# Moving tile addresses in SBUF so that the two operands of each product lie at different residues modulo 256 bytes

## The chip, the cores and the metric

The kernel runs on one core of one Trainium2 chip. A core has five engines with queues of their own: TensorE (PE, matrix products; the profile lists its weight loads as PEld), VectorE (DVE), ScalarE (ACT), GpSimd (POOL) and SyncE (SP, which mostly issues DMAs). On-chip memory is SBUF, 128 partitions, and PSUM, into which TensorE accumulates. The metric is the device time of one execution in microseconds (us).

A product on TensorE has two operands in SBUF. The stationary one (128 columns here) is put into the array by a LDWEIGHTS instruction; the moving one (up to 512 columns) is then streamed past it by a MATMUL. While one MATMUL streams, the LDWEIGHTS of the next one runs beside it.

## What is computed

One layer of a hybrid decoder trunk on 512 tokens of width 1024, in float32:

```python
h = rms_norm(x, g_pre_mix)
z = h @ w_in
y_a = gmlp_mixer(gelu(u), gelu(v), ...)      # spatial gating in chunks of 128 tokens
y_b = nsa_mixer(q, k_cmp, v_cmp, ...)        # 16 heads, 4 KV groups: compressed, selected, window
y_c = rglru_mixer(xr, rg, ...)               # convolution of width 4, linear recurrence
merged = gates[0] * (y_a @ w_br_a) + gates[1] * (y_b @ w_br_b) + gates[2] * (y_c @ w_br_c)
x = x + rms_norm(merged @ w_o, g_post_mix)
f_gate, f_up = split(rms_norm(x, g_pre_ffn) @ w_ffn_in)
return x + rms_norm((silu(f_gate) * f_up) @ w_ffn_out, g_post_ffn)
```

## The kernel before

**Products.** Nearly all the work is matrix products in the type fp32r. Each float32 operand is split into a high part (`hi`, rounded to fp32r by ACT) and a low part (`lo`, the rest, by DVE), by `split` (lines 131 and 136). A product is then three: `hi`x`hi`, `hi`x`lo`, `lo`x`hi`. `passes` (line 259) runs them over the eight blocks of 128 of the inner dimension, with the weight as stationary operand and 512 tokens as moving operand: 24 MATMULs of 512 columns. `v_pair` (line 857) does the opposite: 128 tokens of `hh`/`hl` are stationary, and 256 columns of the weight tile move. Line 614 (`v_half`), line 1496 (`wo_pass`) and line 1876 (`down`) also move weights, in 512 columns. Some large products are done on quarters of the matrices, with sums formed beforehand, in 256 columns: line 1260 (`b_pair`, two of the three branches) and line 1740 (`product_parts`, the FFN's input). Attention uses line 941 (scores: `q` stationary, `K` moving), line 966 (transposes of `P` with `ident`) and line 979 (values: `V` stationary, `ph`/`pl` moving).

**Order.** Python generators are interleaved by `run` and by the planner in `attention`; each yields between small groups of instructions, and so sets the order in which each engine's queue is filled. Waits follow from which tile an instruction reads or writes. In stage 1 (attention) groups of four transposes stand between the products; outside it, products mostly follow one another directly.

**Memory.** SBUF is cut into pools that are laid one behind the other: `const`, `mid` (with the `row` tiles), `stage` (`raw`, where weights land), `merge` (tag `m`), `wts` (the ring of `hi` and `lo`), `big` (tags `y` and `h`), then `early`, and above it a pool for each of three phases. A tile's address is the sum of the sizes ahead of it, each rounded up to 32 bytes. `slab` gives the large tiles. Those with the tags `y`, `mo`, `f` and `wab` are made longer than needed, and the argument `first` shifts the data in them by that many elements. `MOVED` is 16 elements, 64 bytes. With these sizes `mid`, `stage`, `merge`, `wts` and `big` all begin at a multiple of 256 bytes, and their large tiles too. The operands of a product then stand at these distances (address of the moving one minus that of the stationary one, modulo 256):

| product | before |
|---|---|
| 259, 701: `hh`, `gxh`, `yah` with `hi`/`lo` (512 columns) | 0 |
| 614, 1496, 1876 (512 columns, weights move), 498 | 0 |
| 857 `v_pair` (256 columns) | 0 |
| 941 scores, 979 values, 911 | 0 |
| 1260 branches (256 columns): `yc`, `yb`, `t` with `hi`, `lo`, rows | 64, some 192 |
| 259, 1598, 1740 FFN (256 columns): `fh`, `fl`, `t` with `hi`, `lo`, `u` | 64 |
| 259, 1598 with the rows `uh`, `ul` | 192 |

Of the kernel before, what the change touches and what calls it, by code (L numbers as in the profile page):

```python
# [24 lines left out]
F32 = mybir.dt.float32  # L25
F32R = mybir.dt.float32r
# [5 lines left out]
S = 512  # L32
D = 1024
NK = 8
# [18 lines left out]
def hybrid_block(ctx: ExitStack, tc: tile.TileContext, A, out):  # L53
    nc = tc.nc
    V, SC, GP, PE, SY = nc.vector, nc.scalar, nc.gpsimd, nc.tensor, nc.sync

    const = ctx.enter_context(tc.tile_pool(name="const", bufs=1))
# [44 lines left out]
    def slab(name, dt=F32, tag=None, shape=(4, S), first=0):  # L102
        pool, bufs = (merge if tag == "m" else big, TAGS[tag]) if tag in TAGS else phase_pool[tag]
        if tag not in ("y", "mo", "f", "wab"):
            return pool.tile([128, *shape], dt, tag=tag, name=nm(name), bufs=bufs)
        size = 2064 if tag == "f" else 2112
        t = pool.tile([128, size], dt, tag=tag, name=nm(name), bufs=bufs)[:, first:first + math.prod(shape)]
        return t if len(shape) == 1 else t.rearrange(
            "p (a b) -> p a b" if len(shape) == 2 else "p (a b c) -> p a b c", **dict(zip("abc", shape)))
# [28 lines left out]
    res = {}  # L138
# [134 lines left out]
    def const0(shape, name):  # L273
        return phase_pool["s0"][0].tile(shape, F32, name=name, bufs=1)
# [12 lines left out]
    sp4 = const0([128, 8], "sp4")  # L287
    spm8 = const0([128, 8], "spm8")
    lt = const0([128, 6, 8], "lt")
    const0([128, 8], "space")  # L290
    V.memset(ones, 1.0)
    warm = const.tile([128, 17], F32, name="warm")[:, 0:1]
    V.memset(warm, 0.0)
    SC.activation(warm, warm, AF.Exp)
    ident = const.tile([128, 128], F32, name="ident")
# [54 lines left out]

    gh, gl = Pair("gxh", F32R, "y"), Pair("gxl", F32R, "y")
    hh, hl = Pair("hh", F32R, "h"), Pair("hl", F32R, "h")

    def scaled(k):
# [96 lines left out]
    def load_wab():  # L453
        raw = slab("wabr", tag="s1", shape=(2, NK, 128))
        SY.dma_start(raw, A["wab"])
        hi = slab("wabh", F32R, "wab", (2, NK, 128), 48)
        lo = slab("wabl", F32R, "wab", (2, NK, 128), 48)
        wab["hi"], wab["lo"] = hi, lo
        for _ in range(4):
            yield  # L460
        for k in range(0, NK, 2):
            split(raw[:, :, k:k + 2], hi[:, :, k:k + 2], lo[:, :, k:k + 2])
            yield
# [198 lines left out]

    def u_tile(j):
        if j == 0:
            ya["h"], ya["l"] = Pair("yah", F32R, "y"), Pair("yal", F32R, "y")
        g = j // 2
        ps = bank("mm")
        yield from matrix(ps, hh, hl)
        u = row("u")
        gelu2(ps, u)  # L670
        yield
        pm = bank("tr")
        for c in range(4):
            PE.matmul(pm[:, c * 128:(c + 1) * 128], gm["v"][c // 2][:, c % 2, j * 128:(j + 1) * 128],  # L674
                      gm["ws"][:, g, :], start=True, stop=True)
        cb = gm["cb"][:, j % 2:j % 2 + 1]
        rwb = gm["rwb"]
        V.scalar_tensor_tensor(cb[:, 0], rwb[:, 0, g], half[:, 2, j:j + 1], rwb[:, 1, g],
                               op0=OP.mult, op1=OP.add)
        m = row("mix")  # L680
        V.scalar_tensor_tensor(m.rearrange("p (c t) -> p c t", c=4),
                               pm.rearrange("p (c t) -> p c t", c=4), half[:, 1, j:j + 1],
                               cb.to_broadcast([128, 4, 128]), op0=OP.mult, op1=OP.add)
        V.tensor_mul(m, m, u)
        split(m, ya["h"][j], ya["l"][j])
        yield
# [144 lines left out]
        yield  # L831

    def k_tile(g):
        K = slab("K", F32R, "k", (2, 2, S))
        at[g]["k"] = K
        ps = bank("mm")
        yield from matrix(ps, hh, hl)
        for br in range(2):
            src = ps[64 * br:64 * br + 64]
            for h in range(2):  # L840
                SC.activation(K[64 * h:64 * h + 64, 0, br, :], src, AF.Copy)
            for h in range(2):
                V.tensor_sub(K[64 * h:64 * h + 64, 1, br, :], src, f32(K[64 * br:64 * br + 64, 0, br, :]))
        yield

    def v_pair(n):

        us = [unit() for _ in range(2)]
        bs = [bank("mm") for _ in range(2)]
        for c in range(4):  # L850
            q = slice(c * 128, (c + 1) * 128)
            ps = bs[c // 2][:, c % 2 * 256:c % 2 * 256 + 256]
            for k in range(NK):
                hi, lo = us[k // 4]
                ws = slice(k % 4 * 256, k % 4 * 256 + 256)
                for t, (x, w) in enumerate(((hh, hi), (hh, lo), (hl, hi))):
                    PE.matmul(ps, x[k][:, q], w[:, ws], start=(k == 0 and t == 0), stop=(k == NK - 1 and t == 2))  # L857
                if k % 4 == 3:
                    yield
            if c == 1:  # L860
                while n == 1 and 1 not in done:
                    yield
                VV = slab("V", F32R, "v", (4, 2, 2, 2, 64))
                at["v", n] = VV
            if c % 2:
                src = bs[c // 2].rearrange("p (c g b d) -> p c g b d", c=2, g=2, b=2)
                for i in range(2):
                    v = VV[:, c - 1 + i]
                    SC.activation(v[:, :, :, 0, :], src[:, i], AF.Copy)
                    V.tensor_sub(v[:, :, :, 1, :], src[:, i], f32(v[:, :, :, 0, :]))  # L870
# [120 lines left out]
    def mask_in():  # L991
        mask[0] = slab("mask", tag="mask", shape=(S,))
        GP.memset(mask[0], 0.0)
        GP.affine_select(mask[0][:, 384:], mask[0][:, 384:], pattern=[[-1, 128]], compare_op=OP.is_ge,
                         fill=-1e30, base=0, channel_multiplier=1)

    def attention(fills):

# [84 lines left out]

    def yb_tile(name, tag, dt=F32):

        size = {"b1": 2048, "b21": 1024, "b22": 1064}[tag]
        return yb["at"].tile([128, size], dt, tag=tag, name=nm(name), bufs=1)[:, :2048 if tag == "b1" else 1024]

    class Tokens:
# [36 lines left out]
    def yb_rest():  # L1126

        (b11, b12), (b21, b22) = yb["y"].h

        def quarter(t):  # L1130
            return t.rearrange("p (k t) -> p k t", k=4)

        V.tensor_sub(b11, b22, b11)
        yield
        V.scalar_tensor_tensor(b22, b12, -1.0, b22, op0=OP.mult, op1=OP.subtract)
        yield
        t = slab("t", F32R, "f", (2, 4, 256), MOVED)
        yb["b"][2] = t[:, 0], t[:, 1]
        split(b11, *yb["b"][2])
        V.tensor_sub(b21, b21, b11)  # L1140
        yield
        t = yb_tile("t", "b1", F32R).rearrange("p (i k t) -> p i k t", i=2, k=4)
        yb["b"][3] = t[:, 0], t[:, 1]
        split(b22, *yb["b"][3])
        yield
        yb["b"][4] = quarter(yb_tile("t", "b22", F32R)), quarter(slab("t", F32R, "w2", (2048,))[:, :1024])
        split(b21, *yb["b"][4])
        yield
# [101 lines left out]
    def b_pair(p, x="b"):  # L1250
# [39 lines left out]
            return  # L1290
        if p % 2 == 0:
            for n in "hl"[:1 if p else 2]:
                mg.setdefault(n, []).append(slab("m" + n, F32R, "mo"))
        for j, r in ((2 * p, r1), (2 * p + 1, r2)):
            t, m = mg.pop(("b", j)), mg["m"][j]
            V.scalar_tensor_tensor(t, t, 1.0, r, op0=OP.add, op1=OP.mult)
# [6 lines left out]

    def low_late():

        mg["l"].append(slab("ml", F32R, "mo"))
        for j in (4, 5):
            V.tensor_sub(mg["l"][1][:, j - 4], mg["m"][j], f32(mg["h"][1][:, j - 4]))

# [121 lines left out]
    def rows_in():  # L1431
        gb = slab("gb", tag="gb", shape=(2, D))
        res["gb"] = gb
        x = yb_tile("x", "b1").rearrange("p (c n) -> p c n", c=2)
        res["x"] = [x[:, 0], x[:, 1], yb_tile("x", "b21"), yb_tile("x", "b22")]
        res["ss"] = const.tile([128, 4, 4], F32, name="ss")
        fh, fl = res["fh"], res["fl"] = Pair("fh", F32R, "y", MOVED), Pair("fl", F32R, "y", MOVED)
        ff["b"] = {n: (fh.t[h][:, :, q], fl.t[h][:, :, q])
                   for n, h, q in ((11, 0, slice(0, 256)), (21, 1, slice(0, 256)), (22, 1, slice(256, 512)))}

# [130 lines left out]

    def f_split(i):

        t = slab("fs", F32R, "mo" if i == NP - 1 else "y", (2, 2, S))
        for j in range(2):
            ff["h"][2 * i + j], ff["l"][2 * i + j] = t[:, j, 0, :], t[:, j, 1, :]
            split(ff["r"][2 * i + j], t[:, j, 0, :], t[:, j, 1, :])
# [32 lines left out]
    def tokens():  # L1610
# [1 line left out]
        x1, x2 = ff["x", 0], ff["x", 1]  # L1612
        b11, b21, b12, b22 = (x.rearrange("p h k t -> p h (k t)")[:, i] for x in (x1, x2) for i in range(2))
        src = {1: b11, 2: b22, 3: b12, 4: b21}
        t = {n: slab("t", F32R, "mo", (2, 4, 256), MOVED) for n in (1, 2, 3, 4)}
        ff["b"].update({n: (t[n][:, 0], t[n][:, 1]) for n in t})

        def make(n):
# [584 lines left out]
```

## Time and profile before

| | |
|---|---|
| median of 3 runs | 1093.3 us |
| lowest and highest run | 1093.21 and 1093.89 us |
| profiled execution, first to last instruction | 1090.5 us |
| instructions | 16726 |
| mean granted TensorE clock | 0.998 |

The profile is one further execution; it gives its span and no run time of its own, and the median lies 2.8 us above the span. In its rows "128x512 f32 x504" says that a group has 504 instructions with an output of 128 partitions and 512 columns; behind the bar stand the busy time of the group in us and the mean duration of one in ns. A MATMUL's duration runs until its last result is written, while the next one has already begun, so durations add up to more than the span. A row of a list of windows gives the window, TensorE's busy time in it with the number of its instructions, the granted clock, the busy share of the DMA engines and GB/s.

### The profile page before, as it was taken

The numbers are of one execution on the slowest core, as the hardware profiler recorded it, in microseconds if no ns is written. First come the engines' busy times: TensorE is split into PE (matmuls) and PEld (weight loads), VectorE is DVE, ScalarE is ACT, GpSimd is POOL, SyncE is SP. The second block draws the span as 40 slices with busy tenths as digits, with TensorE's granted clock in tenths as the row PEclk, the third lists the DMA queues.
The fourth block names the chain that finished last, engine by engine and source line by source line (L and its number), as shares of the span: only waits on it lengthen the run. The fifth ranks groups of instructions, "written<-read, shape, count | busy, mean of one in ns | idle before, by whom it ended". The sixth has DMA issues, their size and how long they took to land.

```text
span 1090.5 us, 16726 instructions
## 1 busy us (share of the span) xinstructions
PE 1080.7 (99%) x6440; PEld 948.2 (87%) x6440; DVE 883.2 (81%) x1552; ACT 658.9 (60%) x1207; POOL 30.2 (3%) x43
## 2 busy tenths in 40 slices
PE   9999999999999999999999999999999999999997
PEld 7888888999889888898888789988999999998885
DVE  6967779669675899998998887877987888889665
ACT  6757574454444676876777655555656665667552
POOL 1000000000000000000000000000000000022200
PEclk9999999999999999999999999999999999999999
DMA  8332325420322211102111134261323232379902
GB/s 313 104 103 84 97 85 199 182 99 20 116 78 78 78 59 39 59 20 78 59 39 59 58 119 134 76 251 39 117 78 117 100 117 94 135 213 219 185 21 96
DMA packets 34943, 115.06 MB, mean 106 GB/s; under 512 B 3440, under 2 KB 3728, under 8 KB 33968
## 3 DMA queue, kind: packets, MB, share of 16 engines
q1 hardware_dynamic: 28064, 96.93, 26.0%
q0 software_dynamic: 5216, 11.18, 5.1%
q10 hardware_dynamic: 1584, 5.90, 1.4%
q8 instruction: 50, 0.82, 0.3%
q14 instruction: 29, 0.24, 0.1%
HBM read 111.89 MB, written 2.10 MB: 105 GB/s over the span
## 4 chain that ended last, share of the span: by engine, by line
PE 96%; DVE 2%; DMA 1%; ACT 1%; issue 0%; SPq 0%; DVEq 0%; ACTq 0%
PE mm L259 37%; PE mm L1740 16%; PE mm L1876 7%; PE mm L1260 7%; PE mm L1496 4%; PE o L979 4%; PE mm L614 4%; PE sc L941 3%; PE tr L966 3%; PE tr L1876 3%; PE mm L857 2%; PE tr L771 1%; PE tr L498 1%; PE mm L1598 1%; DMA raw<-in_w_v 1%; PE tr L674 1%
## 5 line engine op out<-in xcount | busy, mean ns | idle before, releaser
L259 PE MATMUL mm<-hh,hi 128*128 128x512 f32 x504 | 199.5, 396 | 0.0
L259 PE MATMUL mm<-hh,lo 128*128 128x512 f32 x504 | 197.4, 392 | 0.0
L259 PE MATMUL mm<-hl,hi 128*128 128x512 f32 x504 | 197.0, 391 | 0.0
L136 DVE TENSOR_TENSOR lo<-raw,hi 128x1024 fp32r<-128x1024 f32 (+1 forms) x104 | 121.1, 1164 | 36.9 <-ACT hi L131 34.0
L131 ACT ACTIVATE hi<-raw 128x1024 fp32r<-128x1024 f32 (+1 forms) x104 | 105.2, 1011 | 50.3 <-PE mm L259 18.9
L259 PEld LDWEIGHTS mm<-hh,lo 128*128 128x128 f32 x504 | 94.6, 188 | 19.6
L259 PEld LDWEIGHTS mm<-hl,hi 128*128 128x128 f32 x504 | 94.7, 188 | 18.4 <-issue 0.2
L259 PEld LDWEIGHTS mm<-hh,hi 128*128 128x128 f32 x504 | 94.7, 188 | 18.1 <-PE mm L1260 0.2
L947 ACT ACTIVATE P<-P,ast 128x128 f32<-128x128 f32 (+3 forms) x128 | 70.7, 555 | 23.0 <-DVE ast L945 22.2
L945 DVE CUSTOM_DVE_ANT_0 P<-sc,mask 128x128 f32<-128x128 f32 (+3 forms) x128 | 57.9, 484 | 8.1 <-PE sc L941 7.3
L131 ACT ACTIVATE ph<-tr 128x512 fp32r<-128x512 f32 x80 | 46.9, 592 | 26.2 <-PE tr L966 23.0
L136 DVE TENSOR_TENSOR pl<-tr,ph 128x512 fp32r<-128x512 f32 x80 | 54.4, 686 | 2.9 <-ACT ph L131 0.9
L941 PE MATMUL sc<-K,q 128*128 128x512 f32 (+2 forms) x192 | 51.0, 368 | 0.0
L1740 PE MATMUL mm<-t,hi 128*128 128x256 f32 x288 | 50.7, 276 | 0.0
L1876 PE MATMUL mm<-hi,u 128*128 128x512 f32 x160 | 50.4, 390 | 0.1
L966 PE MATMUL tr<-ident,P 128*128 128x128 f32 x320 | 48.7, 273 | 0.0
L966 PEld LDWEIGHTS tr<-ident,P 128*128 128x128 f32 x320 | 39.1, 140 | 9.6 <-DVE pl L136 1.0
L136 DVE TENSOR_TENSOR lo<-bs,hi 128x1024 fp32r<-128x1024 f32 x28 | 34.1, 1222 | 13.6 <-ACT hi L131 13.5
L1740 PEld LDWEIGHTS mm<-t,hi 128*128 128x128 f32 x288 | 43.3, 188 | 0.0
L1740 PE MATMUL mm<-fh,hi 128*128 128x256 f32 x144 | 40.0, 278 | 0.0
L1740 PE MATMUL mm<-fh,lo 128*128 128x256 f32 x144 | 39.8, 276 | 0.0
L1740 PE MATMUL mm<-fl,hi 128*128 128x256 f32 x144 | 39.8, 276 | 0.0
(474 smaller groups left out, 2895.0 us busy)
## 6 DMA issues: line engine op xcount, KB each, us to landing
raw<-in_w_in SPq DMA_DIRECT2D x64, 512.0 KB, 3.5
rawp<-in_w_fi SPq DMA_DIRECT2D x20, 1024.0 KB, 4.8
bs<-in_w_fo POOLq DMA_DIRECT2D x20, 512.0 KB, 7.4
raw<-in_w_br SPq DMA_DIRECT2D x14, 512.0 KB, 3.5
w<-in_cw ACTq DMA_DIRECT2D x4, 1024.0 KB, 7.3
raw<-in_w_o SPq DMA_DIRECT2D x8, 512.0 KB, 3.9
bs<-in_w_fo SPq DMA_DIRECT2D x8, 512.0 KB, 7.9
raw<-in_w_v SPq DMA_DIRECT2D x7, 512.0 KB, 5.1
```

Of the source, the lines that this page charges most:

```text
L131: res["hi"] = SC.activation(hi, src, AF.Copy)
L136: res["lo"] = V.tensor_sub(lo, src, f32(hi))
L259: res["mm"] = PE.matmul(ps[:m, n0:n1], w[:, k * 128:k * 128 + m], x[k][:, n0:n1], start=(t == 0), stop=(t == 3 * NK - 1))
L614: res["mm"] = PE.matmul(b[c], x[k][:, c * 128:(c + 1) * 128], w[:, kk * 512:kk * 512 + 512], start=(k == 0 and t == 0), stop=(k == NK - 1 ...
L941: PE.matmul(ps[:, :w * n].rearrange("p (b n) -> p b n", b=w), lhs, K[:, i, brs[0]:brs[-1] + 1, :n], start=(i == 0), stop=(i == 1))
L945: V.tensor_tensor_reduce(out=t, in0=ps[:, b * n:b * n + n], in1=mask[0][:, S - n:], scale=-0.125, scalar=3.0e38, op0=OP.add, op1=OP.min, a ...
L947: SC.activation(t, t, AF.Exp, scale=-1.0, bias=st[:, 0, j, b:b + 1], accum_out=st[:, 1, j, b:b + 1])
L966: PE.transpose(pt[:, j * 128:(j + 1) * 128], self.part(j, br)[:, kt * 128:(kt + 1) * 128], ident)
L979: PE.matmul(po, VV[:, kt, g % 2, br].rearrange("p i d -> p (i d)"), x, start=(br == 0 and kt == 0 and t == 0), stop=(br == 1 and kt == a a ...
L1260: res["mm"] = PE.matmul(ps, u[:, k * 128:k * 128 + 128], v[:, k], start=(start and k == t == 0), stop=(k == 3 and t == 2), skip_group_chec ...
L1740: res["mm"] = PE.matmul(ps, w[:, k * 128:k * 128 + 128], x[:, k], start=(start and k == t == 0), stop=(k == 3 and t == 2), skip_group_chec ...
L1876: PE.matmul(ps, a, b, start=id(ps) not in begun, stop=i == len(ops) - 1, skip_group_check=True)
```

## The change

Only sizes, shifts and the order of some allocations are edited. `warm` takes one element instead of 17, which moves `ident` and all pools behind it down by 64 bytes, so that `row`, `raw`, `hi` and `lo` lie at 192 modulo 256. The shifts `first` of the slabs that serve as operands are set anew. An unused tile of 64 bytes (`apart`) stands between the tags `y` and `h`, and another (`aside`) ahead of `K`. The unused tile `space` grows by 64 bytes, so that the slabs of phase 0 behind it lie at 128. `V`'s first slab is allocated in `mask_in`, ahead of `q`, instead of in `v_pair`. Two paddings shrink by 64 bytes (`f`, `b22`), so that all fits.

```diff
-        size = 2064 if tag == "f" else 2112
+        size = 2048 if tag == "f" else 2112
...
-    const0([128, 8], "space")
+    const0([128, 24], "space")
...
-    warm = const.tile([128, 17], F32, name="warm")[:, 0:1]
+    warm = const.tile([128, 1], F32, name="warm")
...
-    gh, gl = Pair("gxh", F32R, "y"), Pair("gxl", F32R, "y")
+    gh, gl = Pair("gxh", F32R, "y", MOVED), Pair("gxl", F32R, "y", MOVED)
+    big.tile([128, MOVED], F32, name="apart")
...
-        hi = slab("wabh", F32R, "wab", (2, NK, 128), 48)
-        lo = slab("wabl", F32R, "wab", (2, NK, 128), 48)
+        hi = slab("wabh", F32R, "wab", (2, NK, 128))
+        lo = slab("wabl", F32R, "wab", (2, NK, 128))
...
-            ya["h"], ya["l"] = Pair("yah", F32R, "y"), Pair("yal", F32R, "y")
+            ya["h"], ya["l"] = Pair("yah", F32R, "y", MOVED), Pair("yal", F32R, "y", MOVED)
...
     def k_tile(g):
+        if g == 0:
+            phase_pool["k"][0].tile([128, MOVED], F32, name="aside")
...
+    def v_slab():
+        return slab("V", F32R, "v", (4, 2, 2, 2, 64))
...
-                VV = slab("V", F32R, "v", (4, 2, 2, 2, 64))
-                at["v", n] = VV
+                VV = at["v", n] = at.get(("v", n)) or v_slab()
...
 def mask_in():
...
+        at["v", 0] = v_slab()
...
-        size = {"b1": 2048, "b21": 1024, "b22": 1064}[tag]
+        size = {"b1": 2048, "b21": 1024, "b22": 1048}[tag]
...
-        t = slab("t", F32R, "f", (2, 4, 256), MOVED)
+        t = slab("t", F32R, "f", (2, 4, 256))
...
-                mg.setdefault(n, []).append(slab("m" + n, F32R, "mo"))
+                mg.setdefault(n, []).append(slab("m" + n, F32R, "mo", first=2 * MOVED))
...
-        mg["l"].append(slab("ml", F32R, "mo"))
+        mg["l"].append(slab("ml", F32R, "mo", first=2 * MOVED))
...
-        fh, fl = res["fh"], res["fl"] = Pair("fh", F32R, "y", MOVED), Pair("fl", F32R, "y", MOVED)
+        fh, fl = res["fh"], res["fl"] = Pair("fh", F32R, "y", 3 * MOVED), Pair("fl", F32R, "y", 3 * MOVED)
...
-        t = slab("fs", F32R, "mo" if i == NP - 1 else "y", (2, 2, S))
+        t = slab("fs", F32R, "mo", (2, 2, S)) if i == NP - 1 else slab("fs", F32R, "y", (2, 2, S), MOVED)
...
-        t = {n: slab("t", F32R, "mo", (2, 4, 256), MOVED) for n in (1, 2, 3, 4)}
+        t = {n: slab("t", F32R, "mo", (2, 4, 256), 2 * MOVED) for n in (1, 2, 3, 4)}
```

By the same addition of sizes the distances become:

| product | before | after |
|---|---|---|
| 259, 701: `hh`, `gxh`, `yah` with `hi`/`lo` | 0 | 64 |
| 614, 857, 1876, 979, 911 | 0 | 192 |
| 498 (`ch` with `wab`), 941 (`K` with `q`) | 0 | 64 |
| 1496 | 0 | 64 or 128 |
| 1260 | 64, some 192 | 64 or 192 |
| FFN with `hi`, `lo` | 64 | 192 |
| FFN with `u` | 64 | 128 |

## The prediction

> **What bounds the kernel now.** I read the page first: the engines, the clock, the chain that ended last.
>
> ```profile
> span 1090.5 us, 16726 instructions
> PE 1080.7 (99%) x6440; PEld 948.2 (87%) x6440; DVE 883.2 (81%) x1552; ACT 658.9 (60%) x1207; POOL 30.2 (3%) x43
> PEclk9999999999999999999999999999999999999999
> PE 96%; DVE 2%; DMA 1%; ACT 1%; issue 0%; SPq 0%; DVEq 0%; ACTq 0%
> PE mm L259 37%; PE mm L1740 16%; PE mm L1876 7%; PE mm L1260 7%; PE mm L1496 4%; PE o L979 4%; PE mm L614 4%; PE sc L941 3%; PE tr L966 3%; PE tr L1876 3%; PE mm L857 2%; PE tr L771 1%; PE tr L498 1%; PE mm L1598 1%; DMA raw<-in_w_v 1%; PE tr L674 1%
> ```
>
> TensorE is busy 99% of the span at full clock in every slice, and 96% of the chain is its own work. Nothing is gained by serving it earlier; the time moves only if a product itself takes a different time. So I next asked for durations. First come the 512-column products in a stage without transposes (line 259, 100 to 200 us), then the 256-column products of the FFN, then those of `v_pair`. The source view gives min/median/max in ns.
>
> ```profile
> L259 PE MATMUL mm<-hh,hi x127: 387/389/478, 99.8 to 198.2; 128*128 128x512 f32 x127
> L259 PE MATMUL mm<-hh,lo x127: 388/389/397, 100.2 to 198.6; 128*128 128x512 f32 x127
> L1740 PE MATMUL mm<-fl,hi 128*128 128x256 f32 x144 | 39.8, 276 | 0.0
> 800.00:960.00 160.00, 159.84 (x1408) 1.00 0.31 113
> L857 PE MATMUL mm<-hi,hh x64: 274/283/363, 342.7 to 490.3; 128*128 128x256 f32 x64
> L857 PE MATMUL mm<-lo,hh x64: 278/283/365, 342.8 to 490.4; 128*128 128x256 f32 x64
> L857 PE MATMUL mm<-hi,hl x64: 278/283/364, 342.9 to 490.5; 128*128 128x256 f32 x64
> L857 PEld LDWEIGHTS mm<-hi,hh x64: 187/192/192, 342.5 to 490.2; 128*128 128x128 f32 x64
> L1740 PEld LDWEIGHTS mm<-fh,hi x117: 187/188/188, 800.1 to 960.0; 128*128 128x128 f32 x117
> ```
>
> Durations overlap, so only differences count. The window 800 to 960 us holds 1408 products in 160 us, 113.6 ns each from start to start, so 276 ns is a pitch of 113 and about 163 of latency. A 512 at 389 then has a pitch of 226, exactly two 256s. Line 857 is the odd one: same shape as line 1740, but 283, 7 ns more, and its weight loads take 192 instead of 188.
>
> Now the addresses, which follow from adding up the tile sizes in the order of allocation (table ahead of this section). Every 512-column product and line 857 read both operands at the same residue; nearly all other 256s are already 64 or 192 apart. So equal residue goes with +7 ns where a product has 256 columns, and with no visible loss where it has 512. My reading: the next weight load runs beside the product, and equal residues lengthen that load by some ns. In a 256 the load fills the whole pitch and sets it; in a 512 it has twice the time and hides.
>
> **The change part by part.** It adds and removes no engine instruction, transfer or wait. Every part is an address, and I price them by product.
>
> *Line 857* goes from 0 apart to 192. It has 3 x 64 = 192 products, each 283 - 276 = 7 ns above the row of line 1740: 192 x 7 = **1.3 us**, all on the path, since nothing beside TensorE sets that stage. Nothing is late next: the reader of the result (ACT, `V`) is simply released earlier.
>
> *The 512-column products* go from 0 apart to 64, 128 or 192. In the undisturbed stage the median is 389 and the maximum 397 to 478, so there is nothing to take away unless 389 itself holds a hidden loss (a rival). But after transposes they run slower for a while:
>
> ```profile
> 609.69 0.60 PE L966 MATMUL tr<-ident,P 128*128 128x128 f32 x4
> 610.04 1.18 PE L941 MATMUL sc<-K,q 128*128 128x512 f32 x4
> 611.06 0.39 PE L259 MATMUL mm<-hh,hi 128*128 128x512 f32 x1
> 611.28 0.39 PE L259 MATMUL mm<-hl,hi 128*128 128x512 f32 x1
> ...
> 613.12 0.39 PE L259 MATMUL mm<-hh,hi 128*128 128x512 f32 x1
> 383.73 0.48 PE L259 MATMUL mm<-hh,hi 128*128 128x512 f32 x1
> L966 PE MATMUL tr<-ident,P 128*128 128x128 f32 x320 | 48.7, 273 | 0.0
> ```
>
> From 610.04 to 613.12 lie 13 products of 512 columns (4 and 9): 3.08 us against 13 x 0.2266 = 2.95, so 0.13 too much. About 0.09 is the first product waiting for its own weights (0.48 instead of 0.39 in the row at 383.73), which no address changes. The other 0.04 us is a transient of some ten products. There are 320 / 4 = 80 such groups, so the transient costs at most 80 x 0.044 = **3.5 us** in all. Is it a matter of the residue? The nearest rows are products that are staggered already and also follow transposes: line 259 with the FFN's `fh`, 64 apart, against line 1598, same operands without transposes between.
>
> ```profile
> L259 PE MATMUL mm<-fh,u x56: 278/279/387, 758.3 to 770.1; 128*128 128x256 f32 x56
> L259 PE MATMUL mm<-fh,ul x4: 281/281/284, 760.7 to 761.8; 128*128 128x256 f32 x4
> L1598 PE MATMUL mm<-fh,u x56: 276/276/276, 775.7 to 785.1; 128*128 128x256 f32 x56
> ```
>
> There a stagger does not prevent the loss after a break: 279 to 281 against 276. So I take nothing for the transient and keep both ends: -3.5 us if the stagger cures it, and a loss if staggered 512s linger as those 256s do (rivals).
>
> *The FFN's 256s* change the distance they have: 64 becomes 192 against the `hi`/`lo` ring and 128 against the units `u`.
>
> ```profile
> L1740 PE MATMUL mm<-t,u 128*128 128x256 f32 x288 | 36.5, 276 | 0.0
> L1740 PE MATMUL mm<-fh,u 128*128 128x256 f32 x192 | 36.5, 276 | 0.0
> L1740 PE MATMUL mm<-fl,u 128*128 128x256 f32 x96 | 26.5, 276 | 0.0
> L1598 PE MATMUL mm<-fh,ul 128*128 128x256 f32 x4 | 1.1, 276 | 0.0
> ```
>
> 192 apart is seen at 276 (the last row: `fh` at 64, `ul` at 128). 128 apart is not in this trace. These 576 products could cost 7 ns more each, 4.0 us, if 128 were like 0, or gain at most the little left over 276; I take 0, since the distances on both sides of 128 give 276.
>
> *Order of allocation*: `V` is now allocated with the mask and lies where `q` did, `q` and `K` move up over the old `vt`. Their first writers come after products that TensorE issues behind the last reader of `vt` (lines 674, then 259), so no new wait: 0. *The transfers* into `raw` now land 192 bytes off a 256-byte line. DMA is 1% of the chain, 11 us at the start; a few per cent of that is 0.3 us at most, taken as 0. *ACT and DVE* read and write shifted tiles; they have 19% and 40% slack and end no chain.
>
> **Sum.** 1090.5 - 1.3 = 1089.2 for the profiled span. The median of the runs is 1093.3, 2.8 us more than the span, which I keep: **1092.0 us**. A measurement of this kernel tells about 0.2%, 2.2 us, from no change, so this forecast counts as "within 0.2%".
>
> **Rivals.**
>
> *1, the transient goes too.* If the conflict in the ten products after a break is between equal residues, the stagger takes up to 3.5 us from the 512s besides the 1.3: 1093.3 - 4.8 = **1088.5**. For it: only equal-residue products show the long wandering transient of the attention stage. Against: the staggered products of line 259 above lose time after a break as well.
>
> *2, the floor of the 512s falls.* 389 might hold the same 7 ns that line 857 shows. By the chain's shares the 512s are about 59 to 62% of the span (lines 259, 1876, 1496, 979, 614, 941), 640 to 680 us at 0.2266, so about 2,900; 2,900 x 7 = 20 us: **1073**. Against it: 389 - 276 = 113, the second half of a 512 costs exactly what a staggered 256 costs; with a hidden 7 ns it would cost 106. The Trainium skill, "TensorE: Matmul & The Clock Gate", section "Back-to-back issue gap", gives N/2.4 + 2.5 ns, 215.8 for 512 columns: by it 2,900 x 11 = 32 us would lie above the floor (an estimate from that page), but it gives 109.2 for 256 as well, which no staggered row here reaches.
>
> *3, no effect.* The 7 ns of line 857 might come from something else than its residues (it is the only 256-column product whose moving operand is a weight tile and whose stationary one is `hh`, and part of it runs inside attention), or the addresses don't come out as said. Then nothing moves: **1093.3**. This is also what the same page states (Part 2, the step on LDWEIGHTS): two independent read ports, so that loading the next weights takes no bandwidth from the running product. The 192 ns of line 857's weight loads against 188 speaks against that rule here.
>
> *4, slower: staggered 512s linger.* At equal residue the transient dies out after some ten products and 389 follows; the staggered 256s of line 259 stayed 3 to 5 ns slow from 758 to 770 us, through some 90 products. If a staggered 512 stays slow in the same way until something jolts it, up to 2,900 x 4 = 11.6 us replace 3.5: 1092.0 + 8 = **1100**. It outweighs the gains when more than about (3.5 + 1.3) / 0.004 = 1,200 products linger, and shows as slower by 0.2% from about 1,750. Against it: in a 512 the weight load has half the pitch to spare, so nothing holds it in that state.
>
> **How the numbers follow.** Forecast 0.45 (own range 1091.0 to 1093.3), rival 1 0.24 (1087.5 to 1091), rival 2 0.05, rival 3 0.10, rival 4 0.16 (1094 to 1101). Faster by over 0.2% (below 1091.1): most of rival 1, rival 2 and a little of the forecast, 0.33; within 0.2%: 0.51; slower: 0.16. The 80% range leaves out rival 2, the edge of rival 1 and the upper half of rival 4: 1087.5 to 1097.0.
>
> **What would show it.** Line 857 at a median of 276 and its weight loads at 188: the first step is right; 283 again: rival 3. Line 259 between 100 and 200 us at 389: no hidden loss; near 382: rival 2. Starts after the transposes spaced by 0.2266 from the second product on: rival 1; medians of 393 in dense stages: rival 4. Line 1740 with `u` above 276: distance 128 costs. Any new wait of TensorE for `K`, `V` or `q` would make the step on allocation wrong.

## The result, and the profile after

The changed kernel takes 1105.82 us (median of 4 runs, 1104.76 to 1106.17), beside 1093.6 us for the kernel before in the same runs: ratio 1.0112, 95% interval 1.0098 to 1.0126. It is slower by 12.2 us. The profiled execution took 1105.64 us with a span of 1103.6, 13.1 more than the span before. In what follows a product is level when its two operands lie at the same residue modulo 256 bytes (distance 0), and staggered at any other distance.

From the page of the changed kernel, the span, the engines, the clock and the chain that ended last:

```profile
span 1103.6 us, 16726 instructions
PE 1094.2 (99%) x6440; PEld 954.9 (87%) x6440; DVE 884.0 (80%) x1552; ACT 660.0 (60%) x1207; POOL 30.1 (3%) x43
PEclk9999999999999999999999999999999999999999
PE 97%; DVE 2%; ACT 0%; DMA 0%; issue 0%; DVEq 0%; ACTq 0%
PE mm L259 36%; PE mm L1746 18%; PE mm L1882 7%; PE mm L1266 7%; PE mm L615 4%; PE mm L1502 4%; PE o L984 4%; PE sc L946 3%; PE tr L971 3%; PE tr L1882 3%; PE mm L863 2%; PE tr L772 1%; PE mm L1604 1%; PE tr L499 1%; PE tr L675 1%; PE tr L884 1%
```

Nothing has become a new bound: the same instructions, the full clock in every slice, the same chain of TensorE's own work (line numbers from 614 on have moved by 1 to 6; the FFN's 1740 is now 1746). TensorE is busy 13.5 us longer with the same 6440 products. So the products themselves take longer. The source view of line 259 between 100 and 200 us (min/median/max in ns), the one that gave 387/389/478 before:

```profile
L259 PE MATMUL mm<-hl,hi x128: 387/392/397, 99.7 to 199.7; 128*128 128x512 f32 x128
L259 PE MATMUL mm<-hh,lo x128: 388/393/398, 99.9 to 199.9; 128*128 128x512 f32 x128
L259 PE MATMUL mm<-hh,hi x127: 388/392/480, 100.2 to 199.4; 128*128 128x512 f32 x127
L259 PEld LDWEIGHTS mm<-hh,lo x127: 187/188/189, 100.4 to 199.7; 128*128 128x128 f32 x127
```

The minimum is where it was within 1 ns, the median has risen by 3 to 4 ns. The weight loads (last row) take 188 ns, as many as in the same view of before. The lists of windows, first the row of the kernel before, then two rows of the changed one (behind TensorE's busy time the number of its instructions):

```profile
100.00:200.00 100.00, 100.00 (x479) 83.94 (x477) 81.65 (x106) 56.89 (x82) 0.54 (x1) 1.00 0.37 127
```

```profile
100.00:200.00 100.00, 100.00 (x471) 83.15 (x470) 80.73 (x106) 57.83 (x84) 0.54 (x1) 1.00 0.37 127
800.00:960.00 160.00, 160.00 (x1385) 160.00 (x1384) 133.83 (x166) 94.69 (x166) 0.00 (x0) 1.00 0.32 108
```

8 of 479 products fewer fit into the first window, and in the FFN (800 to 960 us, 1408 before) 23 fewer. Which of the FFN's are slow, the source view of line 1746 tells:

```profile
L1746 PE MATMUL mm<-t,u x288: 274/281/287, 799.4 to 982.7; 128*128 128x256 f32 x144
L1746 PE MATMUL mm<-fh,u x192: 274/281/285, 798.0 to 981.3; 128*128 128x256 f32 x192
L1746 PE MATMUL mm<-fl,hi x144: 276/276/285, 777.6 to 979.7; 128*128 128x256 f32 x144
```

Those with `u`, now 128 apart, went from 276 to 281; those with `hi`, now 192 apart, stayed. And the same view of line 863 (857 before):

```profile
L863 PEld LDWEIGHTS mm<-hi,hh x64: 187/188/192, 346.7 to 493.9; 128*128 128x128 f32 x64
L863 PE MATMUL mm<-hi,hh x64: 276/276/367, 347.0 to 494.0; 128*128 128x256 f32 x64
```

Here the change did what it says: 283 became 276, the loads 192 became 188. The lines where weights move show the largest rise, from 390 to 395 and 396 (groups, first two of the kernel before, then the same two of the changed one: count, busy us, mean ns):

```profile
L1876 PE MATMUL mm<-hi,u 128*128 128x512 f32 x160 | 50.4, 390 | 0.1
L1876 PE MATMUL mm<-hi,fs 128*128 128x512 f32 x72 | 22.8, 390 | 0.0
```

```profile
L1882 PE MATMUL mm<-hi,u 128*128 128x512 f32 x160 | 51.3, 396 | 0.0
L1882 PE MATMUL mm<-hi,fs 128*128 128x512 f32 x72 | 23.3, 395 | 0.0
```

**Where the 13.1 us are.** For all products of both traces I took the distance from a product's start to the next one's, less the floor for its size, the spacing at which settled products follow one another: 226.7 ns for 512 columns (the level products of line 259 between 100 and 200 us before), 170 for 384 and 113.3 for 256, in proportion. Distances more than 25 ns above the floor (a product behind transposes that waits for its weights, a wait for another engine), together with the other products, are counted apart. Sums in us:

| group | products | before | after |
|---|---|---|---|
| 512 columns, all | 2928 | 3.85 | 12.50 |
| of these lines 259 and 701 with `hh`, `hl` | 1528 | 1.94 | 4.79 |
| of these `down` (moving `hi`/`lo` on `u`, `fs`) | 479 | 0.22 | 3.15 |
| of these `v_half` | 192 | 0.16 | 1.25 |
| 384 columns | 64 | 0.29 | 0.26 |
| 256 columns, all | 2768 | 2.52 | 8.11 |
| of these FFN with `u`, `uh`, `ul` | 768 | 0.42 | 3.72 |
| of these line 857/863 | 192 | 1.17 | 0.27 |
| sum of the small excess | | 6.66 | 20.87 |
| all that is counted apart | | 87.57 | 86.44 |

14.2 us more of small excess, 1.1 less of the rest: 13.1. The rise lies in distances at most 25 ns above the floor, so no longer wait is in it, and the lists of TensorE's waits name `K`, `V` or `q` in neither kernel. By distance the excess per product is:

| columns, distance | before: products, ns | after: products, ns |
|---|---|---|
| 512, 0 | 2802, 1.4 | |
| 512, 64 | | 1887, 3.5 |
| 512, 128 | | 120, 5.7 |
| 512, 192 | | 802, 6.6 |
| 256, 0 | 213, 6.1 | |
| 256, 64 | 2172, 0.5 | 642, 3.4 |
| 256, 128 | | 741, 5.0 |
| 256, 192 | 358, 0.4 | 1364, 1.7 |

At equal residue (0) a 512 loses a few ns for about ten products after a break and then stands on the floor; apart, its mean never comes down. The distances follow from the addresses that the two kernels allocate; the table of distances ahead of the prediction leaves out 240 products of line 1740 that read row tiles as weights, 192 apart before and 64 after.

### The profile page after: what moved, and what is told of

The parts are those of the page before. It is cut to its first block, busy times and chain, and to the rows that moved or that the text cites. A ratio compares the mean times of both kernels' runs of the same rounds, so it can differ in the third digit from the quotient of the medians.

```text
span 1103.6 us, 16726 instructions
## 1 busy us (share of the span) xinstructions
PE 1094.2 (99%) x6440; PEld 954.9 (87%) x6440; DVE 884.0 (80%) x1552; ACT 660.0 (60%) x1207; POOL 30.1 (3%) x43
## 4 chain that ended last, share of the span: by engine, by line
PE 97%; DVE 2%; ACT 0%; DMA 0%; issue 0%; DVEq 0%; ACTq 0%
PE mm L259 36%; PE mm L1746 18%; PE mm L1882 7%; PE mm L1266 7%; PE mm L615 4%; PE mm L1502 4%; PE o L984 4%; PE sc L946 3%; PE tr L971 3%; PE tr L1882 3%; PE mm L863 2%; PE tr L772 1%; PE mm L1604 1%; PE tr L499 1%; PE tr L675 1%; PE tr L884 1%
```

## The experiments

**1. The distance by itself.** 52 series of 48 products behind four transposes each, at 13 distances and two sizes; TensorE is the only engine at work while they run, but for one element that ACT reads behind each series. Experiments 1, 7 and 8 are one execution each.

```diff
+    for n in (512, 256):
+        for d in DIST:   # 0 16 32 64 96 128 160 192 224 256 320 448 512
+            for _ in range(2):
+                turn()
+                ps = series(n, d, 48)
```

> Leaves the whole computation out: 52 series of 48 fp32r products each, 512 columns and then 256, at thirteen distances of the moving from the stationary operand, each series behind four transposes. Theory (distance sets the pitch): at 512 columns the mean duration falls to 389 ns at distance 0 (and 256, 512, if the residue modulo 256 is what counts), and is about 391 at 64 and 395 at 128 and 192; at 256 columns about 283 at 0 and 276 to 281 at 64, 128 and 192. Rival (the loss of the changed kernel comes from its stages, not from the distance): one duration for all distances of a size.

Groups of that run (the name holds the columns and the distance; count, busy us, mean ns; the group of 512 columns at 0 holds the lead-in too and is left out):

```profile
L90 PE MATMUL n512d192x<-x,w 128*128 128x512 f32 x96 | 22.9, 398 | 0.0
L90 PE MATMUL n512d128x<-x,w 128*128 128x512 f32 x96 | 22.8, 396 | 0.0
L90 PE MATMUL n512d64x<-x,w 128*128 128x512 f32 x96 | 22.5, 394 | 0.0
L90 PE MATMUL n512d256x<-x,w 128*128 128x512 f32 x96 | 22.3, 392 | 0.0
...
L90 PE MATMUL n256d256x<-x,w 128*128 128x256 f32 x96 | 12.0, 285 | 0.0
L90 PE MATMUL n256d128x<-x,w 128*128 128x256 f32 x96 | 11.9, 285 | 0.0
L90 PE MATMUL n256d64x<-x,w 128*128 128x256 f32 x96 | 11.8, 282 | 0.0
L90 PE MATMUL n256d192x<-x,w 128*128 128x256 f32 x96 | 11.6, 281 | 0.0
```

The means still hold the first product's wait (about 90 ns in 48). Over the last 30 products of a series the distance from start to start is above the floor by, in ns:

| distance | 0, 256, 512 | 64, 320 | 128 | 160 | 192, 448 | 32, 96, 224 | 16 |
|---|---|---|---|---|---|---|---|
| 512 columns | 0.0 | 2.2 | 5.5 to 6.0 | 7.5 | 6.7 | 6.7 | 4.9 |
| 256 columns | 6.7 | 4.4 | 5.3 to 6.7 | 4.0 | 0.0 or 4.4 | 3.3 to 6.7 | 3.3 to 5.3 |

So the distance modulo 256 changes the pitch with no other engine about, and the two sizes want opposite things: 0 is the best distance for 512 columns and among the worst for 256. For 256 columns the distance doesn't say all: at several distances the two series of a pair settled at different values. At 128 the 256s came out near equal residue and not, as was expected, at 276 to 281 ns. Weighted with the changed kernel's distances this gives its loss without a look at its trace: 1960 x 2.2 + 848 x 6.7 + 120 x 5.8 = 10.7 us for the 512s, less the 3.9 us of transients that the level ones had: 6.8 of the 8.65 us that they rose by. The rest is at 64, where products in the kernel lose 3.5 ns and not 2.2. The trace of the changed kernel shows where the difference lies: in the undisturbed stage from 100 to 200 us line 259 loses 2.4 ns a product, with the same pattern as the series at 64, but the first five of line 259's products behind a break lose 4.6.

**2. `hh` back to equal residue.** The unused tile moves behind `hh` and `hl`.

```diff
-    big.tile([128, MOVED], F32, name="apart")
     hh, hl = Pair("hh", F32R, "h"), Pair("hl", F32R, "h")
+    big.tile([128, MOVED], F32, name="apart")
```

> The changed kernel with the 64-byte tile behind the h slabs instead of ahead of them: hh and hl are level with hi and lo again (distance 0 on line 259 and in v_pair), the FFN's and the output's u units stand at 192, so that the FFN's products with u go from 128 to 192 and the output's products with a stationary u from 192 to 0. Nothing else moves. Theory (distance): line 259 gives back 2.9 us, the FFN with u 3.1, the output 1.9, wo_pass 0.3, v_pair loses 0.9; together 7 us less than the changed kernel, a span of about 1096.5. Rival (the order of allocation, or where transfers land, costs the 12 us): no change, a span of 1103 to 1104.

1096.87 us (1096.01 to 1097.48), ratio to before 1.0043, interval 1.0026 to 1.0059: 4.3 us above before, where the changed kernel was 12.2 above; its span is 9.6 us shorter than that of the changed kernel. From the source view of line 259, 100 to 200 us, and the groups, all of this kernel:

```profile
L259 PE MATMUL mm<-hh,hi x128: 387/389/478, 99.9 to 199.0; 128*128 128x512 f32 x128
L1746 PE MATMUL mm<-t,u 128*128 128x256 f32 x288 | 36.6, 276 | 0.0
L1882 PE MATMUL mm<-hi,u 128*128 128x512 f32 x160 | 50.5, 390 | 0.1
L863 PE MATMUL mm<-hi,hh 128*128 128x256 f32 x64 | 18.3, 286 | 0.0
```

389 is back, at addresses otherwise those of the changed kernel. The step moves more than line 259, because `u` later lies in the same place: `down` is level again, the FFN with `u` goes from 128 to 192, and line 863 falls back to equal residue. In the same sums: `hh` 4.79 to 2.08, `down` with `u` 2.21 to 0.19, FFN with `u` 3.72 to 0.07, line 863 0.27 to 1.10; in all 20.87 to 10.94. That is more than the 7 us expected: 2.0 us of it come from 256s whose distance this step leaves alone, so they stood in another of their states (experiment 6). This run alone therefore doesn't part the 512s from the FFN; experiment 5 does.

**3. `v_half` and part of `fs` level.** The shifts of `gxh`, `gxl` and of the `fs` tiles with the tag `y` are taken out.

```diff
-    gh, gl = Pair("gxh", F32R, "y", MOVED), Pair("gxl", F32R, "y", MOVED)
+    gh, gl = Pair("gxh", F32R, "y"), Pair("gxl", F32R, "y")
...
-slab("fs", F32R, "y", (2, 2, S), MOVED)
+slab("fs", F32R, "y", (2, 2, S))
```

> The changed kernel with gxh, gxl and the y part of fs unshifted, so that v_half's 192 products and about 110 of the output's go from distance 192 to 0. Theory (distance): v_half's median falls from about 395 to 389 ns and gives back 1.1 us, the output's fs products 0.7; together 1.9 us. The stage of cmp_tile(0), which moves gxh past hi, goes from 64 to 0 and gives back 0.05. Rival: medians as in the changed kernel.

A single run, 1104.09 us, 11.5 above the kernel before in the same measurement (1092.59), where the changed kernel was 12.2 above its own; the span is 1.6 shorter than that of the changed kernel. One run doesn't carry so little by itself, but the rows do. Source view of line 615, first of the changed kernel, then of this one:

```profile
L615 PE MATMUL mm<-lo,gxh x64: 393/394/398, 8.4 to 52.0; 128*128 128x512 f32 x64
```

```profile
L615 PE MATMUL mm<-lo,gxh x64: 387/389/393, 8.2 to 51.0; 128*128 128x512 f32 x64
```

The whole group falls by 5 ns, minimum and maximum too: at 192 no product of it stood on the floor. In the sums `v_half` goes from 1.25 to 0.10 us, the products with `fs` from 0.95 to 0.47.

**4. The places alone.** The kernel before with `warm` at one element: everything behind it lies 64 bytes lower, distances unchanged but for 80 products.

```diff
-    warm = const.tile([128, 17], F32, name="warm")[:, 0:1]
+    warm = const.tile([128, 1], F32, name="warm")
```

> The kernel before with its one tile of 68 bytes cut to 4, so that every tile behind it lies 64 bytes lower and all distances between the operands of a product stay as before (80 products excepted, which go from 64 to 128: 0.4 us). Theory (only the distance counts): 1093 to 1094 us with a span of 1090.5 to 1091.5, same as before; the products of line 259 between 100 and 200 us keep a median of 389. Rival (the loss of the change comes from where the tiles lie in themselves: where transfers land, how the reads of ACT and DVE are aligned): a part of the 12 us shows here, over 1096 us.

1093.95 us (1093.18 to 1094.96), ratio 1.0003, interval 0.9994 to 1.0012. Page, and line 259 between 100 and 200 us:

```profile
span 1091.3 us, 16726 instructions
L259 PE MATMUL mm<-hh,lo x127: 388/389/398, 99.7 to 198.1; 128*128 128x512 f32 x127
```

A shift of all these tiles by 64 bytes, and with it where transfers land and how ACT and DVE reads are aligned, costs nothing that can be measured. It is the distance, not the place. The order of allocation is as before here, so this run doesn't test it.

**5. Distance 128 in the FFN alone.** The kernel before, with one 64 bytes more on the FFN's moving operands.

```diff
-Pair("fh", F32R, "y", MOVED), Pair("fl", F32R, "y", MOVED)
+Pair("fh", F32R, "y", 2 * MOVED), Pair("fl", F32R, "y", 2 * MOVED)
...
-slab("t", F32R, "mo", (2, 4, 256), MOVED)
+slab("t", F32R, "mo", (2, 4, 256), 2 * MOVED)
```

> The kernel before with one part of the change alone: the FFN's fh, fl and t move by 64 bytes more, so that 1608 products of 256 columns go from 64 to 128 apart and 264 from 64 to 0. Theory (128 is a bad distance for 256 columns, as the micro-run has it with 5 to 7 ns): 1608 x 5.5 + 264 x 6.7 = 10.6 us, so about 1104 us, and the median of line 1740's products rises from 276 to 281 or 283. Theory as the traces of the two kernels have it (the FFN's products in the changed kernel lose 4 to 5 us in all): 1097 to 1099 us. Rival (the step of the forecast: the distances on both sides of 128 cost nothing, so 128 costs nothing): 1093.3 us, within 0.2%.

1101.35 us (1101.04 to 1102.59), ratio 1.0073, interval 1.006 to 1.0086: 7.8 us slower. From the source view of line 1740, and the windows:

```profile
L1740 PE MATMUL mm<-t,u x288: 274/281/290, 792.6 to 981.0; 128*128 128x256 f32 x144
...
800.00:960.00 160.00, 159.78 (x1347) 159.58 (x1346) 130.04 (x161) 92.73 (x162) 0.00 (x0) 1.00 0.30 103
```

1347 products where there were 1408. The 1602 products at 128 that follow another closely lose 5.3 ns each, those at 0 lose 5.9; in all 9.4 us more of small excess than before, less 0.8 us elsewhere, for a span 8.6 us longer. (The 264 products that went to 0 stood 192 apart before, not 64 as the expectation has it.) The time fell between the two figures given, since they were priced from the micro-run (10.6) and from the changed kernel's sum, which has fewer products at 128. The rival, that 128 costs nothing, is out.

**6. A version meant to beat both.** Before, with the branches' and the FFN's 256s moved from 64 to 192 and the 512s left level.

```diff
-Pair("fh", F32R, "y", MOVED)
+Pair("fh", F32R, "y", 3 * MOVED)
```

(and so for `fl`, `yc`, `yb` and the `mo` slabs of `t`)

> A version that may beat both: the 512-column products stay at equal residue, as before, and 1896 of the 256-column products go from 64 to 192 apart. Theory: both distances have the same two states in the micro-run, one on the floor and one 4.4 ns above it, and the kernel before is on the floor with nearly all of them, so there is at most 1 us to gain: 1092.3 to 1093.5 us, same as before within 0.2%. Rival: at 192 the products are held in the other state, 1896 x 4.4 = 8.3 us, up to 1101 us.

1095.03 us (1094.3 to 1098.33), ratio 1.0017, interval 1.0008 to 1.0025: no gain, a loss near the limit of what can be told. The interval excludes a gain. Groups of this kernel:

```profile
L1740 PE MATMUL mm<-t,hi 128*128 128x256 f32 x288 | 50.9, 277 | 0.0
L1260 PE MATMUL mm<-t,hi 128*128 128x256 f32 x128 | 23.5, 281 | 1.0 <-ACT r L1264 1.0
```

Line 1260 had a mean of 278 before. Some stretches stay 4 to 5 ns above the floor. In the starts of line 1740 from 785 us on, five such stretches (two of some 95 products, three of twelve) open with products 64 apart behind products 192 apart, where one start comes 35 to 115 ns late. Of the other 13 passages from the floor at 192 to 64 there, without a late start, 12 stayed on the floor and one rose. In line 1260 stretches at 64 rise without a late start too. So "64 or 192" is no sufficient rule for 256 columns: at both the same product is found in two states (below).

**7. Own weights or the next ones?** Weights alternate between residues 0 and 64, so that the product's own weights and those loaded beside it differ.

```diff
+    own = lambda i: (64 * (i % 2), 64 * (i % 2))        # residue of weights, of the moving operand
+    nxt = lambda i: (64 * (i % 2), 64 - 64 * (i % 2))
+            series(f"own{n}x", n, 48, own)
+            series(f"next{n}x", n, 48, nxt)
...
+        series("enda", 512, 24, apart(64))
+        series("endb", 512, 24, apart(0))
+        series("endc", 512, 24, apart(192))
```

> Leaves out the whole computation: series of 48 products behind four transposes each, timed by themselves, every series twice. In own512, own256, next512 and next256 the stationary operand alternates between two residues, 0 and 64, so that the product's own weights and the weights loaded while it runs stand at different residues; the moving operand takes the residue of its own weights (own) or of the weights that are loaded next (next). Theory (a product's stream meets the weight load that runs beside it, which is the next one): next512 goes to the floor of 226.7 ns from start to start (median duration 389), own512 stays 2 to 7 ns above it; next256 lies 4 to 7 ns above 113.3 (283), own256 at 276 to 281. Rival (what counts is the product's own weights): the other way round. Second rival (only the addresses of the operands in whole, no pairing): both alike. The other series put sizes and distances in sequence: bya, byb, byc are 24 products of 256 columns at 64, 8 at 192, 24 at 64; if the state of a run of products is kept until something shifts its phase, byc has another excess than bya. enda, endb, endc are 512 columns at 64, at 0, at 192 without a break: if equal residue settles by itself, endb reaches the floor within ten products and the other two do not.

From the source views of the names, and from the timeline (start, us, operation, count):

```profile
L95 PE MATMUL own512x<-x,w x96: 388/394/632, 10.9 to 107.7; 128*128 128x512 f32 x96
L95 PE MATMUL next512x<-x,w x96: 388/395/474, 28.6 to 119.4; 128*128 128x512 f32 x96
L95 PE MATMUL endb<-x,w x48: 387/389/398, 85.3 to 170.5; 128*128 128x512 f32 x48
L95 PE MATMUL byc<-x,w x48: 279/279/282, 56.0 to 138.6; 128*128 128x256 f32 x48
```

```profile
85.31 5.65 PE L95 MATMUL endb<-x,w 128*128 128x512 f32 x24
90.80 5.76 PE L95 MATMUL endc<-x,w 128*128 128x512 f32 x24
96.40 0.60 PE L86 MATMUL turn<-ident,raw 128*128 128x128 f32 x4
```

Theory and rival both fell: neither reaches the floor. Over the last 30 products the two series of `own512` lie 4.9 and 4.8 ns above it and those of `next512` 4.8 and 6.7; `own256` and `next256` are alike as well, 3.3 to 3.4 ns above theirs. The second rival is nearest. What did hold is `endb`: straight behind staggered products, a level series comes to the floor by itself. It takes 5.49 us for 24 (228.8 each, and 226.7 from the eleventh on), while `endc` behind it takes 5.60 (233.3 each) and stays there. `byb`, eight products of 256 columns at 192, went down to the floor; `byc` at 64 behind it went back up, to 117.8.

**8. Who changes.** Only one operand alternates, or both together in blocks of 2, 8 and 16.

```diff
+    def blocks(k):
+        return lambda i: (64 * (i // k % 2), 64 * (i // k % 2))
+        series("level64", 512, 48, lambda i: (64, 64))
+        series("mvturns", 512, 48, lambda i: (0, 64 * (i % 2)))
+        series("stturns", 512, 48, lambda i: (64 * (i % 2), 0))
+        series("both2", 512, 48, blocks(2))
...
+        series("long64", 256, 160, apart(64))
+        series("long192", 256, 160, apart(192))
+        series("then64", 256, 48, apart(64))
```

> Leaves out the whole computation: series of 48 or more products behind four transposes each, every series twice. level64 has both operands at residue 64: if only the distance counts it settles on the floor (226.7 ns from start to start, about 390 a product in the mean). In mvturns the stationary operand stays at 0 and the moving one alternates between 0 and 64, in stturns the reverse; both2, both8, both16 move both operands together every 2, 8 and 16 products, so each product is level in itself. Theory A (a product's own distance counts, and a change of residue starts the transient of some ten products anew): both16 comes to the floor at the ends of its blocks, both8 does not, both2 stays 4 to 5 ns above it as the alternation of the run before did. Theory B (only the distance between a product's stream and the weights loaded beside it counts): stturns equals mvturns, and in both2 two of four products find a level pair in either reading, so it lies under 3 ns in the mean. long64 and long192 are 160 products of 256 columns: 64 stays at 117.8 ns throughout (the run before had it so through 24), 192 drops to 113.3 within eight products and stays; then64 behind it is either kept at 113.3, as in the FFN of the kernel before, or goes back to 117.8, as in the run before. long128 is 96 products of 512 columns 128 apart: they stay 5 to 6 ns above the floor to the end.

The timeline of that run (the three rows `both` are the blocks of 2, 8 and 16, the two rows `long` the distances 64 and 192):

```profile
51.00 11.40 PE L95 MATMUL both<-x,w 128*128 128x512 f32 x48
62.24 0.60 PE L86 MATMUL turn<-ident,raw 128*128 128x128 f32 x4
62.59 11.30 PE L95 MATMUL both<-x,w 128*128 128x512 f32 x48
73.72 0.60 PE L86 MATMUL turn<-ident,raw 128*128 128x128 f32 x4
74.08 11.22 PE L95 MATMUL both<-x,w 128*128 128x512 f32 x48
85.14 0.60 PE L86 MATMUL turn<-ident,raw 128*128 128x128 f32 x4
85.49 19.09 PE L95 MATMUL long<-x,w 128*128 128x256 f32 x160
104.42 0.60 PE L86 MATMUL turn<-ident,raw 128*128 128x128 f32 x4
104.77 18.39 PE L95 MATMUL long<-x,w 128*128 128x256 f32 x160
123.00 5.82 PE L95 MATMUL then<-x,w 128*128 128x256 f32 x48
```

From each start to the next row's, less the first product's 0.09 us: blocks of 2, 11.15 us for 48, 5.6 ns a product above the floor; blocks of 8, 11.04, 3.3; blocks of 16, 10.97, 1.9. Each of these products is level in itself. The rarer the change of residue, the less is lost, as theory A has it; theory B's "under 3 ns" for blocks of 2 is out. A rule by the next load would fit too, if a change of residue costs a transient under it as well. One detail went the other way: some blocks of 8 do reach the floor, after three to five products. `level64` stands on the floor, so level at 64 is as good as level at 0. `mvturns` and `stturns` stay 3 to 6 ns above it. The 256s at 64 keep 117.8 ns through 160 products (18.93 us), at 192 they take 113.4 (18.23), and `then64` is back at 117.8: in a series by itself 64 is not on the floor, though most of the FFN of the kernel before was.

## Why the prediction was wrong

Its likeliest case was 1092.0 us; 1105.8 lies above its range. Step by step:

- **Line 857: right.** Predicted 283 to 276 and loads of 192 to 188; that is what the rows show. It was worth 0.9 us by the starts (1.17 to 0.27), not 1.3, and experiment 2, which takes it back, has a mean of 286 again. The gain is there, and smaller than the losses.
- **The 512-column products: the step that failed.** "So I take nothing for the transient and keep both ends" weighed a transient that a stagger might cure, and took it that a staggered product ends on the same floor as a level one. It doesn't: in the changed kernel it loses 3.5 ns at 64, 5.7 at 128 and 6.6 at 192, and in experiment 1 a loss stays to the end of every staggered series of 512 columns. The sum had nothing for these products; they cost 8.65 us more. The price of the transient itself was nearly right: at most 3.5 us forecast, 3.85 measured before the change for all 512s.
- **Rival 4 came nearest, in mechanism and price.** It said 4 ns on 2,900 products in place of the transients. Measured: 12.5 us on the 2809 products that follow another closely, 4.4 ns each. That the mean came so near is in part luck: the 4 ns were taken from 256-column products, and the losses here run from 3.5 to 6.6 ns by distance. Its "until something jolts it" was not seen: experiment 8 has 96 products at 128 in one series that lose 5.8 ns to the end. It got 0.16 because of the argument against it, "in a 512 the weight load has half the pitch to spare, so nothing holds it in that state". That argument rested on the reading that a longer weight load is the cause. But the loads take 188 ns in level and in staggered 512s alike, so the reading explains line 857's rows at most and can't say what a 512 does.
- **Distance 128 in the FFN: wrong, at the price that was named.** "I take 0, since the distances on both sides of 128 give 276" is an interpolation between two rows in the settled state. 276 became 281. The 576 products that it priced at 4.0 us for the other end lost 2.8; with those of lines 259 and 1598 (1604 after), which it didn't count, the FFN's products with `u` lost 3.3 us in all. Experiment 5 shows it alone: 5.3 ns a product.
- **The other 256s: not foreseen.** 64 to 192 and 192 to 64 were taken as equal, and in settled stretches they are (`fl` with `hi`: 276 and 276). But more stretches stood in the upper state after the change: the remaining 256s lost 3.2 us (8.11 - 2.52 + 0.90 - 3.31), 2.1 of it in the branches. Why, the runs don't show.
- **Order of allocation and transfers at 0: right.** No new wait of TensorE for `K`, `V` or `q`; experiment 4 bounds the effect of the places at 0.12% (the upper end of its interval). The slack that the prediction gives stands the wrong way round: DVE has 19%, ACT 40%. Nothing rests on it.
- **Rival 2, a hidden loss in 389: out.** Level 512s settle at 226.7 ns in every run, and no stretch was found below it. **Rival 3, no effect: out.** The Trainium skill, "TensorE: Matmul & The Clock Gate", Part 2, the step on LDWEIGHTS, says of two independent read ports that loading the next weights doesn't take read bandwidth from the running product. The rows fit it where a level 512 or a settled 256 stands on the floor. Elsewhere the distance of the two operands matters: in experiment 1, with TensorE alone at work, the pitch of a 512 rises by up to 7.5 ns. Whether the weight load is what takes that time is not shown.

The sum closes: 512s +8.65, FFN with `u` +3.3, the other 256s +3.2, line 857 -0.9, waits and the rest -1.1: 13.1 us, the difference of the spans.

What stays open is the mechanism below the residues. That distance and the change of residue matter, and that a level 512 settles, is shown; which of the streams holds up which isn't. Experiment 7 excludes a rule by the distance to the product's own weights alone as well as one by the distance to the next load alone; with the cost of a change of residue added (experiment 8), it can't tell the two apart. Also open is what puts 256s at 64 or 192 on the floor in one stretch and 4 to 5 ns above it in another.

## What to carry to other kernels

Measure a suspected address conflict in a short series for each size of product and each distance before moving anything: a distance among the worst for 256 columns was the best for 512. Read the starts of long undisturbed series and not the first products behind a break, since a loss that dies out after ten products is cheaper than a smaller one that never does. Where a kernel has both sizes, these runs, all with fp32r products, speak for keeping the 512-column operands at equal residue modulo 256 and avoiding 0 and 128 for the 256-column ones.

## What the runs showed of the hardware

- The pitch of an fp32r product depends on the distance of its operands modulo 256 bytes: 226.7 ns at 0, 228.9 at 64, 232.4 at 128, 233.3 at 192 for 512 columns (experiment 1; distances 256 and 512 are as 0, 320 as 64, 448 as 192).
- The loss at level 512s is a transient: some 4 to 9 ns on several of the first ten products after transposes or after staggered ones, then none. Staggered ones repeat a short pattern without end (about -1, 2, 5 ns at 64).
- 256 columns are found in two states at 64 and 192: 113.3 and 117.8 ns. A series at 192 fell to the floor in its first few products in both halves of experiment 8, but in only one of two series of experiment 1; a series at 64 never did in the micro-runs. In the kernel before, FFN products at 64 stood 4 to 5 ns high from 758 to 774 us, came down at products with `uh`, 192 apart, and stayed down through hundreds of products at 64; twelve products with `uh` some 13 us earlier had not brought them down.
